# Differential attention: the value split first in each eviction, the weight split ahead of the second exponential, and weight buffers as rings of single pools

## The chip, the core and the metric

The kernel runs on one core of a Trainium2 chip. The metric is device time of one execution in microseconds; the time before is 2284.65 us, the median of 3 runs (2283.86 to 2284.76). PE stands for TensorE, DVE for VectorE, ACT for ScalarE, POOL for GpSimd, SP for the engine that issues most DMAs. Each engine works through its own instructions in the order in which the program has them; an instruction that waits holds up those behind it on its engine.

## The reference

One decoder layer over 1024 positions of width 1024: a normalised input h feeds three branches (mLSTM, differential attention, cross-attention into 256 memory tokens), whose outputs are projected, gated by sigmoids of h, merged, projected again and added to the input; then a squared-ReLU MLP. The change lies mostly in the second branch, and beside it in where the mLSTM branch and the gates keep their weights.

```python
def diff_attention(q, k, v, q_g, k_g, lam, subln_g, lam_init):
    q = rms_norm(q, q_g)
    k = rms_norm(k, k_g)
    ...
        s = jnp.einsum('bhcqd,bhckd->bhcqk', qblk, kt).astype(jnp.float32) * scale
        s = jnp.where(kpos[None, :] <= qpos[:, None], s, -jnp.inf)
        p = jax.nn.softmax(s, axis=-1)
        a = p[:, :, 0] - lam * p[:, :, 1]
        return jnp.einsum('bhqk,bhkv->bhqv', a.astype(vt.dtype), vt)
    ...
    o = rms_norm(o, subln_g) * (1.0 - lam_init)
```

There are 8 heads; each has two query-key pairs (c = 0 and 1) of 64 columns and values of 128 columns, and the two softmaxes are subtracted with the learned weight lam.

## The kernel before

**Precision.** Every matmul operand is split into a high half in fp32r (a cast on ACT) and a low half (source minus high half, a subtraction on DVE); a product takes three matmuls (high-high, high-low, low-high). So each weight tile, each transposed probability tile and each value tile costs one ACT instruction and one DVE instruction, the second behind the first. `split2` emits such a pair.

**Stages.** Normalisation and memory keys, cross-attention, mLSTM (four heads, 25 weight buffers w, 3 load buffers raw), 96 gate steps of their own (14 weight buffers, 2 load buffers), the attention branch, the rest of the gates, then output projections and the MLP.

**The attention branch (`branch_d`).** Its order is written out by hand and kept on PE, DVE and ACT. Three streams are woven together:

- The projection stream (`d_gemm`) is a generator. One token tile (128 rows by 384 columns: q, k and v of a head) takes 8 steps of three matmuls into one of two PSUM banks (mm). With the eighth step comes `evict`: ACT copies q and k out of the bank (draw, 128x512 with each column block doubled), squares them (dscr) and casts v's high half (dv). The remainder waits in the list `after`: DVE subtracts v's low half out of the bank, then sums the squares (drr). After four tiles POOL makes the reciprocal roots, and `turns` gives four pieces of work: PE transposes the rows of q (twice) and k (twice) into the *other* mm bank (pr), ACT and DVE split the result (dq, dk, dkl). Between the second and third, DVE scales k (four multiplies of draw by drr).
- The attention stream runs in slots s = 0 to 68. A slot computes scores of query block s for c = 0 (PE: sc; DVE: mask and maximum in one instruction, then dst; ACT: the exponential dpe), calls `after()`, combines the two exponentials of block s - 1 on DVE (dpe), runs 4 projection steps, the value products of block s - 2 (po), a piece of `turns`, one more projection step, the scores for c = 1, then the transposes of block s - 1 (tp) whose halves daT are split by ACT and DVE, the second exponential, and the last three projection steps. A head is eight slots, since a block attends to one to eight key blocks. The doS tiles hold the outputs, normalised every four blocks.
- The weight stream (`ahead`) loads and splits a weight of the next head, at the end of each slot: one in six of the eight slots, none in the seventh, two in the eighth. In the last head it loads gate weights instead.

The eighth projection step is the last one of a slot, so an eviction always falls at the slot's end, right before `ahead`.

A tile pool with several buffers is one region of memory: when the pools of a stage are closed and the next stage's are opened over them, a new tile waits for what lies beneath it. `Ring` hands out tiles of several pools in strict turn; before, it is used by the last stages only.

Of the kernel before, what the change touches and what calls it, by code (L numbers as in the profile page):

```python
# [17 lines left out]
P = 128  # L18
# [13 lines left out]
def f32(ap):  # L32
    return ap.bitcast(F32)
# [38 lines left out]
class Layer:  # L72
# [9 lines left out]

    pinned = False
    nmm, kmm = 0, 2
# [17 lines left out]
    def split2(self, hi, lo, src):  # L102

        self.A.copy(hi, src)  # L104
        self.V.tensor_sub(lo, src, f32(hi))  # L105

# [10 lines left out]
    def mm3(self, out, l, r, first, last):  # L117

        mm = self.mm
        mm(out, l[0], r[0], start=first, stop=False)  # L120
        mm(out, l[0], r[1], start=False, stop=False)
        mm(out, l[1], r[0], start=False, stop=last)

    def rsqrt_mean(self, r, ss, width, n):
# [756 lines left out]
    def d_gemm(self, pool, kv):  # L881
# [40 lines left out]

        def evict(ps, i, raws, vh, rr):
            rw = pool.tile([P, 4, 2, 64], F32, tag="draw", name=self.name("draw"))
            A.copy(rw, ps[:, 0:256].rearrange("p (a d) -> p a d", a=4).unsqueeze(2).broadcast_to([P, 4, 2, 64]))
            scr = pool.tile([P, 256], F32, tag="dscr", name=self.name("dscr"))
            A.activation(scr, ps[:, 0:256], AF.Square)
            v = pool.tile([P, 2, P], F32R, tag="dv", name=self.name("dv"))
            A.copy(v[:, 0], ps[:, 256:384])
            raws.append(rw)  # L930
            vh.append(v)

            def rest():
                V.tensor_sub(v[:, 1], ps[:, 256:384], f32(v[:, 0]))
                V.tensor_reduce(rr[:, i], scr.rearrange("p (a d) -> p a d", a=4), axis=AX.X, op=ALU.add)
                if i == 3:
                    rl = rr.rearrange("p a b -> p (a b)")
                    self.rsqrt_mean(rl, rl, 64, 16)
                    self.prep = turns(raws, rr, vh)

            self.after.append(rest)
# [16 lines left out]
    def branch_d(self, pool, dw):  # L958
# [19 lines left out]
        def ahead(tile):  # L978
            for _ in range((1, 1, 1, 1, 1, 1, 0, 2)[tile % 8]):
                if next(dw, 0) is not None:  # L980
                    if self.gate_n < 7 * NK:
                        self.gate_load()
                elif len(self.dw.get(7, ())) == NK:
                    self.gate_fetch(6 * NK)

        def scores(s, c):
# [108 lines left out]
        for n in range(8):  # L1095
            fill(1)
            after()
            fill(3)
            p = self.prep.pop(0) if self.prep else None
            if p:  # L1100
                p[0]()
            fill(4)
            if p:
                p[1]()
            ahead(n)
        for s in range(NS + 5):
# [20 lines left out]
            if more:  # L1127
                exp = scores(s, 1)
            if 1 <= s <= NS:
                hi, lo = turn(s - 1, 0)  # L1130
                hi()
                if more:
                    exp()
                fill(1)
                lo()
                if (s - 1) % 8 >= 4:
                    hi, lo = turn(s - 1, 1)
                    hi()
                    lo()
            else:  # L1140
                if more:
                    exp()
                fill(1)
            fill(2)
            if p:
                p[1]()
            ahead(s)
            if 2 <= s < NS + 2 and i == 3:
# [501 lines left out]
    def run(self):  # L1650
        tc, nc = self.tc, self.nc
        with ExitStack() as ctx:
# [22 lines left out]
            with ExitStack() as c1:  # L1675
# [6 lines left out]
                with ExitStack() as c2:  # L1682
# [11 lines left out]
                    with tc.tile_pool(name="pc", bufs=2) as pc, tc.tile_pool(name="pc1", bufs=1) as pc1, tc.tile_pool(name="pc3", bufs=3) as pc3, tc.tile_pool(name="pc4", bufs=6) as pc4, tc.tile_pool(name="wpc", bufs=8) as self.gwp, tc.tile_pool(name="rpc", bufs=2) as self.grp:  # L1694
# [5 lines left out]
                        self.branch_c(T2())  # L1700
                with tc.tile_pool(name="wpm", bufs=25) as self.wp, tc.tile_pool(name="rpm", bufs=3) as self.rp, tc.tile_pool(name="gm", bufs=1) as gm, tc.tile_pool(name="pm1", bufs=1) as pm1, tc.tile_pool(name="pm", bufs=2) as pm, tc.tile_pool(name="pm3", bufs=3) as pm3:
                    class T3:
                        def tile(_, shape, dt, tag, name):
                            p = pm3 if tag == "pre" else pm if tag in ("tho", "cv", "Ch", "C", "hss", "den") else pm1
                            return p.tile(shape, dt, tag=tag, name=name)
                    self.gpool, self.gwp, self.grp = T3(), self.wp, self.rp
                    self.branch_m(T3(), gm, 1)
                with tc.tile_pool(name="wpg", bufs=14) as self.wp, tc.tile_pool(name="rpg", bufs=2) as self.rp:
                    self.gwp, self.grp = self.wp, self.rp
# [6 lines left out]
                    with tc.tile_pool(name="pd", bufs=2) as pd, tc.tile_pool(name="pd3", bufs=3) as pd3, tc.tile_pool(name="pdm", bufs=1) as pdm, tc.tile_pool(name="pd5", bufs=7) as pd5, tc.tile_pool(name="pdv", bufs=5) as pdv, tc.tile_pool(name="pdv2", bufs=17) as pdv2, tc.tile_pool(name="pd4", bufs=4) as pd4:  # L1716
                        self.tmask = pdm.tile([P, D], F32, name="tmask")
                        nc.gpsimd.memset(self.tmask, 0.0)
# [83 lines left out]
```

## Time and profile before

The profiled execution took 2289.52 us, of which the span of its instructions is 2287.7 us; it is 0.2% over the median of the runs. The page's first part gives the busy time of the engines over that span:

| engine | busy us | share | instructions |
|---|---|---|---|
| PE | 2190.8 | 96% | 11222 |
| DVE | 1395.6 | 61% | 2627 |
| ACT | 1010.7 | 44% | 1994 |
| POOL | 553.7 | 24% | 696 |

By stage (start and end in us of the span): mLSTM 180 to 564, gates 564 to about 640, attention branch with its first projections up to about 1197, the remaining gates to about 1220, projections and MLP to the end. In a row of the timeline stand the start, the duration, engine, line, operation, output and inputs with shapes, the number of instructions merged into it, and in brackets how long the engine had been idle before and what released it. A row of waits gives the waiting instruction, the one it waited for, the sum, the number of times and the longest in us.

### The profile page before, as it was taken

What the parts mean: (1) busy time and instruction counts of PE and PEld (TensorE: products, weight loads), DVE (VectorE), ACT (ScalarE), POOL (GpSimd) and SP (SyncE); (2) the same over time, 40 slices, a digit from 0 to 9 for tenths busy, and PEclk for the clock granted to TensorE, in tenths of its full rate; (3) what the DMA queues carried; (4) which work ended last, traced back from release to release, by engine and by line L of the source; (5) the groups of instructions that cost most, each with busy time, mean ns of one, the idle gap of its engine ahead of it and who ended that gap; (6) DMA issues with size and microseconds to landing.
All of it is one profiled execution on the core that took longest, in us unless ns stands there. A gap on an engine that the chain in (4) does not pass through costs nothing.

```text
span 2287.7 us, 30543 instructions
## 1 busy us (share of the span) xinstructions
PE 2190.8 (96%) x11222; PEld 1881.3 (82%) x11222; DVE 1395.6 (61%) x2627; ACT 1010.7 (44%) x1994; POOL 553.7 (24%) x696
## 2 busy tenths in 40 slices
PE   7999999999999999999999999999999999899999
PEld 5788789888898888988887888887787888688777
DVE  6635457553137777777753133453588777766678
ACT  6533445443246666666553111223445444542332
POOL 2100000000011111111100002202566665565553
PEclk9999999999999999999999999999999999899999
DMA  6023212211311111110125344435535444854344
GB/s 242 24 79 97 80 52 79 77 35 48 126 44 33 30 34 38 31 38 23 39 87 190 115 126 137 148 107 178 175 110 194 153 153 151 303 175 151 126 142 166
DMA packets 113780, 247.89 MB, mean 108 GB/s; under 512 B 11065, under 2 KB 19550, under 8 KB 111582
## 3 DMA queue, kind: packets, MB, share of 16 engines
q1 hardware_dynamic: 111326, 233.36, 31.1%
q10 hardware_dynamic: 2304, 12.58, 1.3%
q8 instruction: 88, 1.44, 0.3%
q14 instruction: 62, 0.51, 0.1%
HBM read 178.76 MB, written 67.14 MB: 107 GB/s over the span
## 4 chain that ended last, share of the span: by engine, by line
PE 59%; DVE 18%; DMA 9%; ACT 8%; issue 3%; POOL 2%; SPq 0%; ACTq 0%; DVEq 0%; POOLq 0%
PE mm L91 35%; PE p L91 18%; DVE sc L67 3%; PE sc L91 3%; ACT dpe L67 3%; DVE dst L67 2%; PE tp L94 1%; DMA wraw<-in_wdown 1%; DVE dpe L67 1%; DVE w L67 1%; DVE wo L105 1%; PE po L91 1%; DMA xd<-r_d 1%; DMA kraw<-y 1%; ACT draw L67 1%
## 5 line engine op out<-in xcount | busy, mean ns | idle before, releaser
L91 PE MATMUL mm<-hT,w 128*128 128x512 f32 x1920 | 465.1, 396 | 3.5 <-ACT w L104 2.7
L91 PE MATMUL mm<-w,hT 128*128 128x384 f32 (+3 forms) x2496 | 459.8, 331 | 2.5 <-ACT w L111 2.2
L91 PEld LDWEIGHTS mm<-hT,w 128*128 128x128 f32 x1920 | 354.4, 189 | 79.5 <-ACT w L104 4.3
L91 PEld LDWEIGHTS mm<-w,hT 128*128 128x128 f32 x2496 | 390.6, 189 | 12.1 <-ACT w L111 2.8
L91 PE MATMUL p<-xd,wo 128*128 128x512 f32 x1344 | 314.2, 395 | 16.9 <-DVE acc L1598 9.4
L91 PEld LDWEIGHTS p<-xd,wo 128*128 128x128 f32 x1344 | 254.2, 190 | 76.8 <-DVE acc L1598 12.3
L91 PE MATMUL p<-xo,wo 128*128 128x512 f32 x1344 | 310.0, 392 | 6.0 <-DVE st L1452 4.0
L91 PEld LDWEIGHTS p<-xo,wo 128*128 128x128 f32 x1344 | 253.5, 189 | 61.1 <-ACT pt L1265 4.4
L91 PE MATMUL mm<-kt,w 128*128 128x512 f32 x1152 | 261.6, 389 | 0.5 <-DVE w L112 0.5
L91 PEld LDWEIGHTS mm<-kt,w 128*128 128x128 f32 x1152 | 216.1, 188 | 46.0 <-DVE w L112 1.0
L104 ACT CAST wo<-wraw 128x896 fp32r<-128x896 f32 x122 | 114.9, 942 | 189.7 <-PE p L91 116.8
L105 DVE TENSOR_TENSOR wo<-wraw,wo 128x896 fp32r<-128x896 f32 x122 | 145.9, 1211 | 49.8 <-ACT wo L104 49.7
L67 ACT ACTIVATE dpe<-sc,dst,drr 128x256 f32<-128x256 f32 (+7 forms) x128 | 106.5, 832 | 139.5 <-DVE dst L67 139.3
L1179 POOL TENSOR_TENSOR wraw<-wraw 128x128 f32<-128x128 f32 x128 | 98.1, 766 | 211.4 <-DMA wraw<-in_wdown 132.9
L111 ACT CAST w<-raw 128x256 fp32r<-128x256 f32 (+2 forms) x144 | 86.6, 620 | 132.1 <-PE mm L91 116.3
L112 DVE TENSOR_TENSOR w<-raw,w 128x256 fp32r<-128x256 f32 (+2 forms) x144 | 100.7, 719 | 49.1 <-ACT w L111 48.9
L105 DVE TENSOR_TENSOR xd<-xd 128x1536 fp32r<-128x1536 f32 (+2 forms) x36 | 69.1, 1924 | 72.3 <-ACT xd L104 72.0
L1180 POOL TENSOR_TENSOR wraw<-wraw 128x128 f32<-128x128 f32 x128 | 101.1, 790 | 0.0
L127 POOL TENSOR_SCALAR hss<-hss 128x4 f32<-128x4 f32 x8 | 3.3, 410 | 396.5 <-ACT mscr L755 273.5
L67 DVE CUSTOM_DVE_ANT_0 sc<-sc,tmask 128x256 f32<-128x256 f32 (+7 forms) x128 | 97.0, 758 | 3.0 <-PE sc L91 2.4
L67 DVE TENSOR_TENSOR w<-raw,w 128x384 fp32r<-128x384 f32 (+1 forms) x88 | 44.0, 508 | 85.1 <-ACT w L67 85.0
L1181 POOL TENSOR_TENSOR wraw<-wraw 128x128 f32<-128x128 f32 x128 | 92.8, 725 | 0.0
(324 smaller groups left out, 3187.4 us busy)
## 6 DMA issues: line engine op xcount, KB each, us to landing
wraw<-in_wup SPq DMA_DIRECT2D x64, 256.0 KB, 3.2
r_d<-xts SPq DMA_DIRECT2D x16, 1024.0 KB, 4.3
wraw<-in_wdown SPq DMA_DIRECT2D x64, 256.0 KB, 3.0
xd<-r_d SPq DMA_DIRECT2D x19, 768.0 KB, 7.1
xd<-r_d SPq DMA_DIRECT2D x14, 1024.0 KB, 6.5
raw<-in_wgate SPq DMA_DIRECT2D x48, 256.0 KB, 3.1
gates<-gt SPq DMA_DIRECT2D x48, 256.0 KB, 2.0
raw<-in_wd SPq DMA_DIRECT2D x32, 384.0 KB, 3.1
```

What stands on the lines that cost most here:

```text
L67: return self.tc.keep_in_program_order(f(*a, **k))
L91: self.pin(self.nc.tensor.matmul(out, l, r, start=start, stop=stop))
L94: self.pin(self.nc.tensor.transpose(out, x, self.ident))
L104: self.A.copy(hi, src)
L105: self.V.tensor_sub(lo, src, f32(hi))
L111: nc.scalar.copy(hi, src)
L112: nc.vector.tensor_sub(lo, src, f32(hi))
L127: g.tensor_scalar(r, ss, 1.0 / width, EPS, op0=ALU.mult, op1=ALU.add)
L1179: G.tensor_add(r[:, 4], r[:, 0], r[:, 3])
L1180: G.tensor_sub(r[:, 5], r[:, 4], r[:, 1])
L1181: G.tensor_sub(r[:, 6], r[:, 1], r[:, 0])
```

## The change

In `evict`, the value tile is split first, cast and subtraction together, before q and k are copied and squared; the subtraction is no longer in `after`. In a slot, `ahead` moves from the end to before the second exponential; from there until after the probability tile's low half, the low halves that `split2` would emit are collected (`defer`) and emitted by `lows`. In the eight slots that only project, `ahead` moves two steps forward. The weight and load buffers of mLSTM and of the gates become rings of pools with one buffer each; for the gates they are opened as load buffers, mask, weights, with the weights handed out from the other end, and the mask of the attention branch lies in that group.

```diff
     def split2(self, hi, lo, src):

         self.A.copy(hi, src)
-        self.V.tensor_sub(lo, src, f32(hi))
+        low = lambda: self.V.tensor_sub(lo, src, f32(hi))
+        if self.defer is None:
+            low()
+        else:
+            self.defer.append(low)
...
+    @contextmanager
+    def rings(self, *spec):
+
+        with ExitStack() as c:
+            yield [
+                Ring([c.enter_context(self.tc.tile_pool(name=f"{n}{i}", bufs=1)) for i in range(k)]) for n, k in spec
+            ]
...
         def evict(ps, i, raws, vh, rr):
+            v = pool.tile([P, 2, P], F32R, tag="dv", name=self.name("dv"))
+            self.split2(v[:, 0], v[:, 1], ps[:, 256:384])
             rw = pool.tile([P, 4, 2, 64], F32, tag="draw", name=self.name("draw"))
             A.copy(rw, ps[:, 0:256].rearrange("p (a d) -> p a d", a=4).unsqueeze(2).broadcast_to([P, 4, 2, 64]))
             scr = pool.tile([P, 256], F32, tag="dscr", name=self.name("dscr"))
             A.activation(scr, ps[:, 0:256], AF.Square)
-            v = pool.tile([P, 2, P], F32R, tag="dv", name=self.name("dv"))
-            A.copy(v[:, 0], ps[:, 256:384])
             raws.append(rw)
             vh.append(v)

             def rest():
-                V.tensor_sub(v[:, 1], ps[:, 256:384], f32(v[:, 0]))
                 V.tensor_reduce(rr[:, i], scr.rearrange("p (a d) -> p a d", a=4), axis=AX.X, op=ALU.add)
...
+        def lows():
+            d, self.defer = self.defer, None
+            for f in d:
+                f()
...
-            fill(4)
+            fill(2)
+            ahead(n)
+            fill(2)
             if p:
                 p[1]()
-            ahead(n)
...
+            self.defer = []
             if 1 <= s <= NS:
                 hi, lo = turn(s - 1, 0)
                 hi()
+                ahead(s)
                 if more:
                     exp()
                 fill(1)
                 lo()
+                lows()
                 if (s - 1) % 8 >= 4:
                     hi, lo = turn(s - 1, 1)
                     hi()
                     lo()
             else:
+                ahead(s)
                 if more:
                     exp()
                 fill(1)
+                lows()
             fill(2)
             if p:
                 p[1]()
-            ahead(s)
...
-                with tc.tile_pool(name="wpm", bufs=25) as self.wp, tc.tile_pool(name="rpm", bufs=3) as self.rp, ...
+                with self.rings(("wpm", 25), ("rpm", 3)) as (self.wp, self.rp), ...
...
-                with tc.tile_pool(name="wpg", bufs=14) as self.wp, tc.tile_pool(name="rpg", bufs=2) as self.rp:
+                with self.rings(("rpg", 2), ("ptm", 1), ("wpg", 14)) as (self.rp, ptm, self.wp):
+                    self.wp.pools.reverse()
...
-                        self.tmask = pdm.tile([P, D], F32, name="tmask")
+                        self.tmask = ptm.tile([P, D], F32, name="tmask")
```

On DVE, in the slot of the attention loop that splits a daT tile of 384 columns (ISA is the mask maximum with its read-out; sc the scores, dst the maxima and sums, dpe the exponentials, w a weight, dv the value tile, drr the sums of squares). Before:

```order
L67 TENSOR_TENSOR daT_8905<-tp_8901,daT_8905 128x384
L67 TENSOR_TENSOR w_8924<-raw_8676,w_8924 128x384
L67 ISA sc_8930,dst_8929<-sc_8930,tmask 128x640
L67 ISA dst_8929 128x1
L67 SCALAR_TENSOR_TENSOR dst_8929<-dst_8929,drr_8204 128x1
L67 TENSOR_TENSOR dv_8922<-mm_8865,dv_8922 128x128
L67 TENSOR_REDUCE drr_8590<-dscr_8920 128x4
L67 RECIPROCAL dst_8853<-dst_8853 128x2
```

and now:

```order
L67 TENSOR_TENSOR daT_9054<-tp_9050,daT_9054 128x384
L67 TENSOR_TENSOR w_9056<-raw_8800,w_9056 128x384
L67 TENSOR_TENSOR dv_9070<-mm_9014,dv_9070 128x128
L67 ISA sc_9080,dst_9079<-sc_9080,tmask 128x640
L67 ISA dst_9079 128x1
L67 SCALAR_TENSOR_TENSOR dst_9079<-dst_9079,drr_8353 128x1
L67 TENSOR_REDUCE drr_8739<-dscr_9075 128x4
L67 RECIPROCAL dst_9003<-dst_9003 128x2
```

The value tile's subtraction has moved from behind the mask maximum to ahead of it; the weight's subtraction keeps its place, though its cast on ACT now comes earlier.

On ACT, in the same slot (doS is an output tile, dk a transposed key tile). Before:

```order
L67 CAST daT_8905<-tp_8901 128x384
L67 ACTIVATE dpe_8852,dst_8853<-sc_8896,dst_8853,drr_7846 128x512
L67 COPY draw_8918<-mm_8865 128x512
L67 ACTIVATE dscr_8920<-mm_8865 128x256
L67 CAST dv_8922<-mm_8865 128x128
L67 CAST w_8924<-raw_8676 128x384
L67 ACTIVATE dpe_8927,dst_8929<-sc_8930,dst_8929,drr_8204 128x640
```

and now:

```order
L67 CAST daT_9054<-tp_9050 128x384
L67 CAST w_9056<-raw_8800 128x384
L67 ACTIVATE dpe_9002,dst_9003<-sc_9045,dst_9003,drr_7995 128x512
L67 CAST dv_9070<-mm_9014 128x128
L67 COPY draw_9073<-mm_9014 128x512
L67 ACTIVATE dscr_9075<-mm_9014 128x256
L67 ACTIVATE dpe_9077,dst_9079<-sc_9080,dst_9079,drr_8353 128x640
```

The weight's cast stands ahead of the second exponential, and the value tile is cast before q and k are copied. In the new program the copy draw waits for DVE's subtraction of the value tile.

On ACT, where mLSTM's last head ends and the first gate weights of the next stage are cast (tho is the output gate, Ch the state's high half, gt a gate tile). Before:

```order
L779 ACTIVATE tho_5324<-mm_5299 128x512
L111 CAST Ch_5382<-C_5380 128x258
L750 ACTIVATE den_5385<-sc_5370 128x1
L753 ACTIVATE hS_5368<-sc_5370,den_5385 128x256
L755 ACTIVATE mscr_5390,hss_5369<-hS_5368 128x256
L111 CAST Ch_5416<-C_5414 128x258
```

and now:

```order
L791 ACTIVATE tho_5402<-mm_5377 128x512
L104 CAST w_5744<-raw_5740 128x256
L104 CAST w_5747<-raw_5740 128x256
L104 CAST w_5752<-raw_5742 128x256
L104 CAST w_5755<-raw_5742 128x256
L115 CAST Ch_5460<-C_5458 128x258
L762 ACTIVATE den_5463<-sc_5448 128x1
L765 ACTIVATE hS_5446<-sc_5448,den_5463 128x256
```

The casts of the gate weights, which stood 20 rows later behind the stage's last gate tiles, have moved in between the last output gate and the last chunks' state; on DVE their subtractions stand likewise ahead of the state update C.

More of the change, by code (lines that the diff above doesn't have):

```diff
@@ L1 @@
 import math
-from contextlib import ExitStack
+from contextlib import ExitStack, contextmanager
 import numpy as np
@@ L80, in name @@
         return f"{s}_{self.n}"
-    pinned = False
+    pinned, defer = False, None
     nmm, kmm = 0, 2
@@ L1700, in run @@
                         self.branch_c(T2())
-                with tc.tile_pool(name="wpm", bufs=25) as self.wp, tc.tile_pool(name="rpm", bufs=3) as self.rp, tc.tile_pool(name="gm", bufs=1) as gm, tc.tile_pool(name="pm1", bufs=1) as pm1, tc.tile_pool(name="pm", bufs=2) as pm, tc.tile_pool(name="pm3", bufs=3) as pm3:
+                with self.rings(("wpm", 25), ("rpm", 3)) as (self.wp, self.rp), tc.tile_pool(name="gm", bufs=1) as gm, tc.tile_pool(name="pm1", bufs=1) as pm1, tc.tile_pool(name="pm", bufs=2) as pm, tc.tile_pool(name="pm3", bufs=3) as pm3:
                     class T3:
```

## The prediction

> **What bounds the kernel now.** I read the page's busy shares first, then busy time by stretch, then what TensorE (PE) waited for in the attention stage, then its order of time.
>
> ```profile
> PE 2190.8 (96%) x11222; PEld 1881.3 (82%) x11222; DVE 1395.6 (61%) x2627; ACT 1010.7 (44%) x1994; POOL 553.7 (24%) x696
> ...
> core 0: us, PE busy (x) PEld busy (x) DVE busy (x) ACT busy (x) POOL busy (x), PEclk, DMA share, GB/s
> 250.00:564.00 314.00, 311.53 (x1828) 273.71 (x1829) 172.70 (x431) 147.76 (x409) 12.20 (x16) 0.99 0.19 60
> 564.00:575.00 11.00, 8.20 (x37) 5.49 (x36) 4.33 (x10) 4.98 (x11) 0.47 (x1) 1.00 0.63 187
> 675.00:1135.00 460.00, 429.88 (x2768) 411.86 (x2767) 358.32 (x973) 283.08 (x685) 70.97 (x55) 1.00 0.11 33
> 1480.00:2287.00 807.00, 776.00 (x3367) 633.25 (x3365) 570.20 (x639) 324.59 (x401) 412.92 (x540) 0.98 0.48 163
> ...
> PE pr L94 <- DVE dv L67: 28.6, 39, 1.0
> PE tp L94 <- DVE doS L67: 3.2, 8, 0.5
> PE mm L91 <- ACT w L104: 2.7, 2, 2.4
> ```
>
> PE is busy for 2190.8 of 2287.7 us, so all the idle that any reordering can win back is 96.9 us. The stretches say where it lies: 30.1 us in the differential-attention loop (460.00 - 429.88), 2.8 us where mLSTM hands over to the gates (564 to 575), 2.5 us inside mLSTM, 31 us in the output projections and MLP, which the diff does not touch. In the attention loop PE's clock is 1.00, so it is stalls and not throttling. The three waits name them: 39 times the transposes of q or k (pr) stand until VectorE (DVE) has finished the low half of v, 28.6 us in all; 8 times the transposes of the weights (tp) stand for DVE's doS, 3.2 us; twice the gates' matmuls stand for a weight cast, 2.7 us. One slot in order of time shows why v is late (ACT is ScalarE; the mask maximum is sc<-sc,tmask):
>
> ```profile
> 889.57 0.55 DVE L67 TENSOR_TENSOR daT<-tp,daT 128x384 fp32r<-128x384 f32 x1
> 889.75 0.78 ACT L67 ACTIVATE dpe<-sc,dst,drr 128x512 f32<-128x512 f32 x1 [1.12 <-DVE dst L67]
> 890.42 0.19 ACT L67 ACTIVATION_READ_ACCUMULATOR dpe<-sc,dst,drr 128x1 f32 x1
> 890.51 0.57 ACT L67 COPY draw<-mm 128x512 f32<-128x512 f32 x1
> 890.98 0.39 ACT L67 ACTIVATE dscr<-mm 128x256 f32<-128x256 f32 x1
> 891.25 0.27 ACT L67 CAST dv<-mm 128x128 fp32r<-128x128 f32 x1
> 891.40 0.54 ACT L67 CAST w<-raw 128x384 fp32r<-128x384 f32 x1
> 891.98 0.56 DVE L67 TENSOR_TENSOR w<-raw,w 128x384 fp32r<-128x384 f32 x1 [1.86 <-ACT w L67]
> 892.29 0.80 PE L91 MATMUL po<-dv,daT 128*128 128x256 f32 x6
> 892.45 0.82 DVE L67 CUSTOM_DVE_ANT_0 sc<-sc,tmask 128x640 f32<-128x640 f32 x1
> 893.45 0.28 DVE L67 TENSOR_TENSOR dv<-mm,dv 128x128 fp32r<-128x128 f32 x1
> 893.88 0.63 PE L94 MATMUL pr<-ident,draw 128*128 128x128 f32 x4 [0.78 <-DVE dv L67]
> 894.42 0.75 DVE L67 SCALAR_TENSOR_TENSOR dpe<-dpe,dst,dpe 128x512 f32<-128x512 f32 x1
> 895.93 0.63 PE L94 MATMUL tp<-ident,dpe 128*128 128x128 f32 x4
> ```
>
> ACT drains the finished bank in the order draw, dscr, v, then casts a weight. DVE, in order, idles 1.86 us for that cast, subtracts the weight, does the mask maximum, and only then reads v's low half out of the bank (893.45 to 893.73). PE has ended its value products at 893.09 and needs that same bank for pr: 0.78 us lost.
>
> **Attention loop, part by part.** No instruction is added or removed; their order changes. *Weight split ahead of the second exponential.* ACT sat idle 1.12 us before that exponential (waiting for DVE's dst), the cast takes 0.54 us: it costs nothing on ACT while that gap exceeds 0.54 us, and at most the 0.54 us beyond it. Its subtraction (0.56) follows daT on DVE: 889.57 + 0.55 = 890.12, done by about 890.65, in DVE's former 1.86 us of idle. Its weight load is issued from the same step; SP's order in this loop is unchanged, so no load is passed. *Value first.* v's cast takes draw's place, 890.51 to 890.78; its subtraction follows, about 890.84 to 891.12 (gaps of some 0.06, as between the 891.40 cast's end and 891.98). The mask maximum then starts at about 891.05 instead of 892.45, 1.4 us sooner, and the chain behind it, which also loses v's place in the middle (about 0.2), brings the combination (dpe) from 894.42 to about 892.8. In exchange draw waits for the subtraction, as the new program's waits show: 891.18 instead of 890.51, 0.67 us later; dscr ends near 892.05. The bank is free at 892.05 instead of 893.73, before PE's 893.09. The whole 0.78 us goes here, and the next thing PE needs, tp, would come at 895.93 - 0.78 = 895.15, with its operand ready at 892.8 + 0.75 = 893.6.
>
> The Trainium skill, PSUM — Partial Sum Buffer, section "PSUM bank collisions raise a hardware error", states that ACT and DVE must be kept apart on one bank, two reads included; by that rule the split's round trip through DVE is a price of the change (rival B). Were the two reads allowed together, draw would start at 890.78 here and the sum would stay, since pr is then bound by PE's 893.09; no run here shows such an overlap.
>
> Not each slot has this room. In a slot that also scales k, DVE has four multiplies:
>
> ```profile
> 875.36 1.42 DVE L67 TENSOR_TENSOR draw<-draw,drr 128x256 f32<-128x256 f32 x4
> 877.35 0.56 DVE L67 TENSOR_TENSOR w<-raw,w 128x384 fp32r<-128x384 f32 x1 [0.57 <-ACT w L67]
> 877.82 0.56 DVE L67 CUSTOM_DVE_ANT_0 sc<-sc,tmask 128x384 f32<-128x384 f32 x1
> 878.98 0.63 PE L94 MATMUL pr<-ident,draw 128*128 128x128 f32 x4 [0.76 <-DVE dv L67]
> 879.52 0.48 DVE L67 SCALAR_TENSOR_TENSOR dpe<-dpe,dst,dpe 128x256 f32<-128x256 f32 x1
> 880.32 0.38 PE L94 MATMUL tp<-ident,dpe 128*128 128x128 f32 x2
> ```
>
> Now weight and v come first, then the multiplies (about 876.4 to 877.85), then the maximum at about 877.8, as before. Only v's 0.2 us leaves the chain: the combination ends near 879.8 instead of 880.00. With pr unblocked PE would want tp at 880.32 - 0.76 = 879.56, so some 0.25 us of this wait comes back at tp. Two slots of each eight-slot head are of this kind: 16 x 0.25 = 4.0 us. The doS wait stands in the last slot of a head,
>
> ```profile
> 930.22 0.66 PE L94 MATMUL tp<-ident,dpe 128*128 128x128 f32 x4 [0.38 <-DVE doS L67]
> ```
>
> behind the same late maximum (there DVE subtracts two weights), so it goes too. Sum for the loop: 28.6 + 3.2 - 4.0 = 27.8 us. Bounds: 31.8 (nothing comes back) and about 12 (rival A).
>
> **mLSTM to gates.** Before, the first gate weights could not be loaded until PE was done with the stage; single buffers let them start when the two or three buffers beneath are free, by the program's waits after the last output-gate tile.
>
> ```profile
> 537.99 0.60 ACT L779 ACTIVATE tho<-mm 128x512 f32<-128x512 f32 x1 [4.31 <-PE mm L91]
> 541.09 0.48 DVE L743 SCALAR_TENSOR_TENSOR C<-C,g_dec,sc 128x258 f32<-128x258 f32 x1 [6.68 <-PE sc L91]
> 544.39 0.52 PE L91 MATMUL sc<-Ch,qp 128*128 128x258 f32 x3
> 564.14 0.33 SPq L435 DMA_DIRECT2D raw<-in_wgate  x1
> 567.39 2.12 PE L91 MATMUL mm<-hT,w 128*128 128x512 f32 x8 [2.40 <-ACT w L104]
> 569.77 30.50 PE L91 MATMUL mm<-hT,w 128*128 128x512 f32 x130 [0.26 <-ACT w L104]
> ...
> raw<-in_wgate SPq DMA_DIRECT2D x48, 256.0 KB, 3.1
> ...
> L104 ACT CAST w<-raw 128x256 fp32r<-128x256 f32 x64 | 23.3, 404 | 21.1 <-DMA raw<-in_wgate 18.2 <-PE mm L91 2.9
> ```
>
> The load moves from 564.14 to about 537.8, so PE's 2.40 + 0.26 = 2.7 us go. But the casts and their subtractions now stand ahead of the state update C and its cast Ch: landing 3.1 us after 537.8, four splits of 0.4 us end near 542.7, C slips from 541.09 to 542.7 and Ch's low half is ready near 544.1, against PE's 544.39. The next update, behind four more splits, misses by perhaps 0.3 us. I take 0.7 us given back, net 2.0 (bounds: 2.7 gained, 1.0 lost if landings take 1 us longer twice).
>
> **Inside mLSTM** the buffers now come round in strict turn. The order differs only at the first head switch: eight weight casts move from among the state chunks to behind the tile that last uses the old weights.
>
> ```profile
> 283.14 0.57 ACT L640 COPY pre<-mm 128x512 f32<-128x512 f32 x1
> ...
> 302.13 0.58 ACT L640 COPY pre<-mm 128x512 f32<-128x512 f32 x1
> ```
>
> The first row drains that last tile, the second the first tile of the new weights. At PE's pace of about 0.24 us a matmul (2.12 us for eight overlapping ones, above) its 24 matmuls and the chunks between them begin near 294, so the casts have some 10 us in hand: zero, bounds 0 to 3 us lost. The mask's own pool and one load moved by a place behind the loop touch no wait of PE: zero.
>
> **Sum.** 27.8 + 2.0 = 29.8 us. The profiled execution took 2289.52 us (2287.7 of span and 1.8 around it), 4.9 us over the median of the runs; it should become 2259.7, and the median 2284.65 - 29.8 = **2255 us**.
>
> **Rivals.** *A: the combination takes the wait's place.* If the DVE chain does not move forward, PE stops at tp instead of pr and keeps only the slack that stood before tp: 0.32 us in the k-scaling slot (880.32 against 879.52 + 0.48), 0.76 in the other. At 0.3 us for each of 39 waits that is 12 us, with the 2.0 of the handover 2284.65 - 14 = 2271 us. For it: in the k-scaling slots exactly this holds. Against it: DVE's 1.86 us of idle ahead of the maximum. *B, slower: the round trip of v.* ACT's draw stands for DVE's subtraction, and dscr, the first exponential and pr stand behind draw. The price is the 0.67 us above in each of 64 slots, 43 us, against 31.8 us of waits gone: 2284.65 + 43 - 32 - 2 = 2294 us. It decides only from the point where dscr ends after PE's value products, 1.0 us later than the walk has it (892.05 against 893.09); DVE would have to be that much further behind at each eviction, and the walk finds it free. *C: PE's stalls go, but the handover and the ring cost their bounds* (1.0 and 3 us lost): 2284.65 - 27.8 + 4 = 2261. *D: the order does not do what it says*: excluded for the place of the casts, which the program fixes.
>
> **How the numbers follow.** Forecast (24 to 34 us gained, C included) 0.80; A and halfway to it 0.13; B 0.03; no change for a reason not seen 0.02; more than 34 us, if removing a stall also saves PE's restart, 0.02. The forecast's own range is 2250 to 2261; reaching towards A until no more than 0.2 is left out, and with a little beyond the upper bound of the gain, 2249 to 2268. A measurement of this kernel tells about 0.2% (4.6 us) from no change: faster 0.95, same 0.02, slower 0.03.
>
> **What would show it.** Right: the pr waits for dv near zero, DVE's idle for ACT w in this loop mostly gone, a head taking some 60 us instead of 64, small tp waits for dpe in two slots a head, no 2.4 us wait for a gate weight, PE idle 1 to 5 us in the loop. Wrong: pr waiting for ACT's dscr (B), tp waiting for dpe in most slots (A), waits for Ch or mpT before 564, or ACT's weight casts waiting for their loads, which would hold every exponential behind them.

## The result, and the profile after

The changed kernel takes 2249.8 us (median of 4 runs, 2249.61 to 2250.31), beside 2284.7 us (2283.86 to 2287.53) for the kernel before: 34.9 us less, a ratio of 0.9845 with an interval of 0.9828 to 0.9863. The prediction was 2255 us, with 2249 to 2268 as its range. So the direction and most of the size came as forecast (29.8 of 34.9 us). Two things did not: the gain is 5.1 us larger than the sum, and the experiments put it on another half of the change than the sum's working did.

The busy shares of the page and then the busy time in the attention loop after the change, with the same columns as before (length, PE, PEld, DVE, ACT and POOL busy with their counts, granted clock, DMA share, GB/s):

```profile
PE 2182.6 (97%) x11222; PEld 1877.5 (84%) x11222; DVE 1398.3 (62%) x2627; ACT 1019.8 (45%) x1994; POOL 540.4 (24%) x696
```

```profile
651.71:1107.66 455.95, 453.06 (x2932) 436.22 (x2931) 377.05 (x1017) 304.34 (x719) 66.72 (x60) 1.00 0.12 35
```

This stretch, called the loop below, runs from the first transposition of q or k (pr) to the last. The same stretch of the kernel before:

```profile
653.31:1144.18 490.87, 458.95 (x2931) 438.45 (x2932) 374.00 (x1017) 296.27 (x719) 75.69 (x60) 1.00 0.12 33
```

The loop is 34.92 us shorter. 29.03 us of this is PE's idle time (31.92 before, 2.89 after: length less busy time). The other 5.89 us is PE's *busy* time, 458.95 against 453.06, for the same matmuls at the same clock. What PE still waits for in this loop:

```profile
PE tp L94 <- DVE dpe L67: 1.6, 7, 0.2
PE tp L94 <- DVE doS L67: 1.3, 6, 0.3
```

No pr wait is left, and no wait of the gates' matmuls for a weight cast (before 28.6 and 2.7 us). A head now takes 59.5 us in place of 64.3 (from the value products of one slot to those of the same slot of the next head). One slot in order of time, the one that the prediction walked through; its value products (po) start at 871.95 here and at 892.29 before:

```profile
868.17 0.52 ACT L67 CAST w<-raw 128x384 fp32r<-128x384 f32 x1
869.23 0.78 ACT L67 ACTIVATE dpe<-sc,dst,drr 128x512 f32<-128x512 f32 x1 [0.54 <-DVE dst L67]
869.52 0.55 DVE L67 TENSOR_TENSOR w<-raw,w 128x384 fp32r<-128x384 f32 x1
870.00 0.25 ACT L67 CAST dv<-mm 128x128 fp32r<-128x128 f32 x1
870.29 0.29 DVE L67 TENSOR_TENSOR dv<-mm,dv 128x128 fp32r<-128x128 f32 x1 [0.22 <-ACT dv L67]
870.49 0.82 DVE L67 CUSTOM_DVE_ANT_0 sc<-sc,tmask 128x640 f32<-128x640 f32 x1
870.61 0.59 ACT L67 COPY draw<-mm 128x512 f32<-128x512 f32 x1 [0.36 <-DVE dv L67]
871.95 0.80 PE L91 MATMUL po<-dv,daT 128*128 128x256 f32 x6
872.30 0.78 DVE L67 SCALAR_TENSOR_TENSOR dpe<-dpe,dst,dpe 128x512 f32<-128x512 f32 x1
872.59 0.62 PE L94 MATMUL pr<-ident,draw 128*128 128x128 f32 x4
874.65 0.62 PE L94 MATMUL tp<-ident,dpe 128*128 128x128 f32 x4
```

Counted from po's start, the mask maximum comes at -1.46 us (before +0.16), the combination of the exponentials at +0.35 (before +2.13), pr at +0.64 (before +1.59). The weight's cast fits into ACT's gap ahead of the second exponential: the gap is 0.54 us where it was 1.12. The order of events is the predicted one. But pr came 0.95 us sooner, and the wait shown for it before was only 0.78. The rest is overlap: po ends at 871.95 + 0.80 = 872.75 by its row, and pr starts 0.16 us ahead of that end, where before it started 0.78 us behind it.

### The profile page after: what moved, and what is told of

Same layout as the page of the kernel before. It is cut to its first block, busy times and chain, and to the rows that moved or that the text cites. A ratio compares the mean times of both kernels' runs of the same rounds, so it can differ in the third digit from the quotient of the medians.

```text
span 2247.8 us, 30530 instructions
## 1 busy us (share of the span) xinstructions
PE 2182.6 (97%) x11222; PEld 1877.5 (84%) x11222; DVE 1398.3 (62%) x2627; ACT 1019.8 (45%) x1994; POOL 540.4 (24%) x696
## 4 chain that ended last, share of the span: by engine, by line
PE 68%; DVE 14%; DMA 8%; ACT 5%; issue 2%; POOL 2%; SPq 0%; DVEq 0%; ACTq 0%; POOLq 0%
PE mm L91 40%; PE p L91 18%; PE sc L91 4%; PE tp L94 2%; PE po L91 2%; DVE sc L67 1%; DMA wraw<-in_wdown 1%; ACT dpe L67 1%; DVE wo L105 1%; DVE dpe L67 1%; PE pr L94 1%; DVE draw L67 1%; DVE dst L67 1%; DMA xr<-h_d 1%; DVE w L116 1%
## 5 line engine op out<-in xcount | busy, mean ns | idle before, releaser
L104 ACT CAST xd<-xd 128x1536 fp32r<-128x1536 f32 (+2 forms) x36 | 54.9, 1528 | 73.0 <-DMA xd<-r_d 73.0
```

## The experiments

Times of one kernel spread over 2.6 to 14 us from run to run in these comparisons, so kernels that differ by less than some 4 us are not told apart by their times. The length of the loop in the trace, from the first pr to the last, repeats much better: 490.87, 491.51 and 490.89 us in three kernels with the loop of before, and 455.95, 456.01, 455.69 and 455.67 us in four with the changed loop. It is the main reading in what follows (the times come from several comparisons, each with its own runs of the kernel before; the ratios in the text are taken within one):

| kernel | loop us | PE idle in it | PE busy in it | waits of pr and tp listed in it | time us |
|---|---|---|---|---|---|
| before | 490.87 | 31.92 | 458.95 | pr 39, tp 7 | 2284.7 |
| value split first alone | 511.37 | 45.43 | 465.94 | pr 1, tp 43 | 2301.8 |
| value cast first alone | 490.89 | 31.94 | 458.95 | pr 39, tp 7 | 2284.6 |
| weight split early alone | 452.27 | 0.61 | 451.66 | none | 2246.0 |
| the change | 455.95 | 2.89 | 453.06 | tp 13 | 2249.8 |
| the change, value's subtraction late | 452.50 | 0.75 | 451.75 | none | 2245.1 |
| the change, value last | 474.43 | 14.73 | 459.70 | tp 20 | 2260.5 |
| the change, k scaled one slot sooner | 450.84 | 0.41 | 450.43 | tp 1 | 2240.2 |

The list of waits holds those of 0.15 us and more. The eighth doS wait of the kernel before (0.32 us at 1210.82) lies behind the loop.

### Each half of the attention change alone

The kernel before, with only the value split moved:

```diff
         def evict(ps, i, raws, vh, rr):
+            v = pool.tile([P, 2, P], F32R, tag="dv", name=self.name("dv"))
+            self.split2(v[:, 0], v[:, 1], ps[:, 256:384])
             rw = pool.tile(...)
...
             def rest():
-                V.tensor_sub(v[:, 1], ps[:, 256:384], f32(v[:, 0]))
```

> The kernel before with the value split first alone: cast and subtraction at once, before q and k are copied; the weight split stays at the slot's end. Theory (the late weight split holds the mask maximum, the early value only frees the bank): pr no longer waits for dv, but the combination is no earlier than before (0.2 us sooner without the value in its chain, some 0.3 later since the weight cast now follows the round trip), so PE stops at tp and keeps only the slack of 0.3 us in most of 39 slots: about 2273 us (2268 to 2277), with some 20 us of tp waits. Rival (the bank alone held PE): 2252 us and hardly a tp wait.

Measured: 2301.82 us (2300.47 to 2303.28), ratio 1.0079 (1.0061 to 1.0098): slower than the kernel before of the same comparison (2283.11), by 18.7 us. The expectation of 2273 fell, and its rival of 2252 with it. Its waits of PE in the attention loop:

```profile
PE tp L94 <- DVE dpe L67: 26.3, 30, 1.2
PE tp L94 <- DVE doS L67: 18.7, 13, 2.1
```

The pr waits are gone and 45.0 us of tp waits stand in their place. The same slot in this kernel, one head sooner:

```profile
827.95 0.29 DVE L67 TENSOR_TENSOR dv<-mm,dv 128x128 fp32r<-128x128 f32 x1 [0.69 <-ACT dv L67]
828.27 0.59 ACT L67 COPY draw<-mm 128x512 f32<-128x512 f32 x1 [0.36 <-DVE dv L67]
829.03 0.52 ACT L67 CAST w<-raw 128x384 fp32r<-128x384 f32 x1
829.22 0.80 PE L91 MATMUL po<-dv,daT 128*128 128x256 f32 x6
829.58 0.56 DVE L67 TENSOR_TENSOR w<-raw,w 128x384 fp32r<-128x384 f32 x1 [1.34 <-ACT w L67]
829.86 0.62 PE L94 MATMUL pr<-ident,draw 128*128 128x128 f32 x4
830.05 0.82 DVE L67 CUSTOM_DVE_ANT_0 sc<-sc,tmask 128x640 f32<-128x640 f32 x1
832.93 0.66 PE L94 MATMUL tp<-ident,dpe 128*128 128x128 f32 x4 [0.86 <-DVE doS L67]
```

pr follows po by 0.64 us, unhindered. But the mask maximum comes at +0.83 us after po's start, 0.67 later than before (+0.16). DVE still waits 1.34 us for the weight's cast, which ACT now makes behind the eviction *and* behind the round trip of v, and the mask maximum stands behind the weight's subtraction. tp comes at +3.71, where it came at +3.64 before and at +2.70 in the changed kernel. This is rival A, the combination taking the wait's place, with rival B's round trip on top, paid not at pr but at tp.

This slot is hardly longer for it: from po to the next po it takes 8.54 us, beside 8.47 before. The loss lies in others. The slot behind it, which had no wait before, goes from 7.83 to 8.56 us; the last slot of a head, where two weights are split, goes from 9.53 to 10.2 us, with a tp wait of 2.1. In four of these seven last slots it is 11.8 us instead, at a granted clock of 0.86 (1066.06 to 1077.84), beside 10.2 us at 1.00 (863.56 to 873.75): 4 x 1.6 = 6.4 of the 20.5 us that the loop is longer are clock. Each of these dips follows a tp wait of 2.1 us, but two such waits (734.44 and 868.93) are followed by none, so what brings them is not shown.

The other half, everything of the change in the slot loop (`ahead` moved, `defer`, `lows`) with `evict` and the pools as they were:

> The kernel before with the weight split ahead of the second exponential alone: value last in the eviction, its subtraction behind the mask maximum as before. Theory: the maximum starts some 1.8 us sooner, so the subtraction behind it also ends before PE's value products in most slots; only the two k-scaling slots of a head keep about 0.3 us: 2254 to 2258 us, pr waits of about 5 us. Rival (the value's place decides): the pr waits stay near 28 us and the time near 2284 us.

Measured: 2246.02 us (2240.06 to 2249.75), ratio 0.9833 (0.9808 to 0.9858). It carries the whole gain of the loop. The expectation, 2254 to 2258 us with 5 us of pr waits, was too slow: the k-scaling slots keep no wait either. The loop, in which the trace lists no wait:

```profile
649.22:1101.49 452.27, 451.66 (x2932) 437.00 (x2931) 374.45 (x1016) 300.17 (x719) 75.63 (x60) 1.00 0.12 35
```

In its walked slot:

```profile
864.71 0.55 DVE L67 TENSOR_TENSOR w<-raw,w 128x384 fp32r<-128x384 f32 x1
...
865.50 0.83 DVE L67 CUSTOM_DVE_ANT_0 sc<-sc,tmask 128x640 f32<-128x640 f32 x1 [0.24 <-PE sc L91]
...
866.50 0.28 DVE L67 TENSOR_TENSOR dv<-mm,dv 128x128 fp32r<-128x128 f32 x1
...
867.43 0.80 PE L91 MATMUL po<-dv,daT 128*128 128x256 f32 x6
```

With the weight's subtraction out of the way, the mask maximum starts 1.93 us ahead of po and now waits for PE's scores. v's subtraction, still behind it, is done at 866.78, ahead of po's start and 1.29 us ahead of pr (868.07). The value never had to go first: it was late only because the mask maximum ahead of it was late, and that because of the weight. That the change is slower than this half alone rests on the loops (455.95 against 452.27; 455.69 in the change with the old pools, below); the times do not tell them apart.

### The value's place, with the weight early

Three kernels vary the place of the value. In the first, ACT casts v first as in the change, and DVE subtracts in `after` again:

```diff
-            self.split2(v[:, 0], v[:, 1], ps[:, 256:384])
+            A.copy(v[:, 0], ps[:, 256:384])
...
             def rest():
+                V.tensor_sub(v[:, 1], ps[:, 256:384], f32(v[:, 0]))
```

> The changed kernel with the value's cast first but its subtraction back behind the mask maximum, so draw waits for no other engine. Theory (what counts is that DVE no longer waits for a weight cast): the subtraction still ends ahead of pr except in the k-scaling slots, 2252 to 2256 us, pr waits 2 to 6 us. Rival (the subtraction must stand ahead of the maximum): 2265 us or more.

2245.06 us (2242.21 to 2249.13), ratio 0.9832 (0.9816 to 0.9849); loop 452.50 us, no wait listed. The 2252 to 2256 us with 2 to 6 us of pr waits that were expected did not come, nor did the rival's 2265. The same as the weight alone: the 3.5 us between this and the change's 455.95 are what the immediate subtraction costs.

In the second, v is split last in the eviction, with its subtraction at once:

```diff
         def evict(ps, i, raws, vh, rr):
-            v = pool.tile([P, 2, P], F32R, tag="dv", name=self.name("dv"))
-            self.split2(v[:, 0], v[:, 1], ps[:, 256:384])
...
             A.activation(scr, ps[:, 0:256], AF.Square)
+            v = pool.tile([P, 2, P], F32R, tag="dv", name=self.name("dv"))
+            self.split2(v[:, 0], v[:, 1], ps[:, 256:384])
```

> The changed kernel with the eviction in the order draw, dscr, value: cast and subtraction together but last, so no copy waits for DVE, and the maximum waits for the value's cast. Theory: the maximum starts some 0.7 us later than in the changed kernel; slots with slack hide it, the k-scaling slots and a few others lose 0.5 to 0.9 us at tp: 2258 to 2265 us with 8 to 14 us of tp waits. Rival (the round trip of draw through DVE is what costs): faster than 2249.8 us.

2260.46 us (2256.86 to 2262.07), ratio 0.9892 (0.9877 to 0.9907), as expected; loop 474.43 us. Two rows of a slot, and then its waits of PE in this loop:

```profile
888.03 0.29 DVE L67 TENSOR_TENSOR dv<-mm,dv 128x128 fp32r<-128x128 f32 x1 [0.95 <-ACT dv L67]
888.24 0.96 DVE L67 CUSTOM_DVE_ANT_0 sc<-sc,tmask 128x768 f32<-128x768 f32 x1
```

```profile
PE tp L94 <- DVE dpe L67: 11.0, 14, 1.0
PE tp L94 <- DVE doS L67: 3.2, 6, 0.5
```

A DVE instruction that stands ahead of the mask maximum and waits for ACT delays tp here, v's subtraction as well as the weight's. If the subtraction is to be immediate, v has to be first; if it is late, v may stand first or last.

The last of this kind settles whether ACT's order or DVE's made "value first alone" slow: the kernel before, with ACT's cast of v ahead of draw and nothing else moved.

> Kernel before, with only the cast of v's high half moved ahead of draw on ScalarE; the subtraction of its low half stays behind the mask maximum on VectorE, and the weight split stays behind the evictions. Theory: the place of a VectorE instruction in its order decides, because it stands ahead of the mask maximum; ScalarE's order of the same three drains does not. Without the subtraction between them the three drains and the weight cast end where they did (no 0.67 us round trip), so the mask maximum starts where it did and v's low half is read where it was: first to last q or k transposition 490 to 492 us as in the kernel before (490.87, and 491.51 with the rings), some 39 waits of pr for v's low half, 28 to 29 us in all, time within 5 us of the kernel before. Rival: that splitting the value first alone came out slower lies in ScalarE's order (draw and its square later for every consumer); then this kernel shows the tp waits of that one (some 45 us) and a loop near 511 us.

2284.62 us (2281.74 to 2293.31), ratio 0.9997 (0.9985 to 1.0009); loop 490.89 us, with these waits (of the whole execution, so that the doS wait behind the loop is among them):

```profile
PE pr L94 <- DVE dv L67: 28.6, 39, 1.0
PE tp L94 <- DVE doS L67: 3.0, 8, 0.5
```

The loop is as long as before to 0.02 us, as expected. ACT's order alone changes nothing; the 20.5 us by which the loop of "value first alone" is longer come with DVE's subtraction in the middle of the eviction.

### The k scaling

The change's remaining waits begin in the slot that scales k, where four multiplies stand ahead of the mask maximum:

```profile
857.63 1.42 DVE L67 TENSOR_TENSOR draw<-draw,drr 128x256 f32<-128x256 f32 x4
858.97 0.56 DVE L67 CUSTOM_DVE_ANT_0 sc<-sc,tmask 128x384 f32<-128x384 f32 x1
859.12 0.34 PE L91 MATMUL po<-dv,daT 128*128 128x256 f32 x2
860.48 0.48 DVE L67 SCALAR_TENSOR_TENSOR dpe<-dpe,dst,dpe 128x256 f32<-128x256 f32 x1
861.02 0.44 PE L94 MATMUL tp<-ident,dpe 128*128 128x128 f32 x2 [0.22 <-DVE dpe L67]
```

First edit: the multiplies ahead of the slot's last two projection steps in the program.

```diff
-            fill(2)
             if p:
                 p[1]()
+            fill(2)
```

> The changed kernel with the four k multiplies issued ahead of the last projection steps, so that on DVE they stand ahead of the value's subtraction in two slots of eight; draw then waits some 1.4 us longer. This moves the eviction past the point at which the round trip (rival B) decides. Theory: in the shorter of the two slots dscr ends some 0.7 us after PE's value products, pr waits for ACT; 16 slots lose 0.2 to 0.8 us: 2253 to 2258 us, pr waits of 4 to 7 us. Rival (the round trip is always hidden): 2249 to 2251 us.

2246.4 us (2244.16 to 2250.88), ratio 0.9835 (0.982 to 0.985); loop 455.24 us, 0.7 less than the change: nothing that the time can show. The expected 2253 to 2258 us did not come. The multiplies are as many and still stand ahead of the mask maximum; only v's subtraction changed sides with them. The theory holds in kind, not in size: the 7 tp waits for dpe are gone, and in their place stand 6 waits of pr for ACT's dscr, 1.1 us in all instead of the 4 to 7 expected. So the round trip (rival B) does reach pr once v's subtraction stands 1.4 us later, and costs little there.

Second edit: the multiplies a whole slot sooner, behind the first q piece rather than the second, where sixteen value products give DVE room.

```diff
-            return [(lambda: q_(0), none), (lambda: q_(1), scale), ...
+            return [(lambda: q_(0), scale), (lambda: q_(1), none), ...
```

> The changed kernel with the four k multiplies one slot earlier (with the first q piece instead of the second), into slots whose combination has over 1 us of slack before tp. Theory (a stall costs its shown idle plus about 0.13 us of matmul tail that no longer overlaps): the 7 waits of 0.22 us for dpe go, 7 x 0.35 = 2.5 us: 2247.4 us, provided POOL's roots are done in time. Rival (a stall costs its idle alone): 2248.2 us. Other rival (the multiplies only move the wait): 2249.8 us with 0.2 us waits in other slots.

2240.17 us (2239.2 to 2247.04), ratio 0.9824 (0.9797 to 0.9852). The expected time was 2247.4. The changed kernel again, in the same comparison:

> The changed kernel once more, on the chip of the next two: 2249.8 us (2249 to 2251).

2248.24 us (2247.19 to 2249.78), ratio 0.9853 (0.9822 to 0.9883). The loop of the edit:

```profile
648.02:1098.86 450.84, 450.43 (x2932) 436.30 (x2931) 377.97 (x1017) 304.68 (x719) 66.71 (x60) 1.00 0.12 35
```

5.17 us shorter than the repetition's 456.01, about twice the 2.5 us expected, with one wait of 0.4 us left. The mask maximum of that slot now starts 1.50 us ahead of po, where it started 0.15 ahead. The doS waits of the head's last slot went as well; that they were lag carried over from the k-scaling slot fits this, but was not tested apart. It has the lowest median and the shortest loop here. The intervals of the two ratios overlap, so the gain over the change rests on the loop.

Third, the normalisation of the outputs moved ahead of the value products as well (the call of `norm` in the slot loop):

> The same, and the transposes of the normalised outputs moved ahead of the value products, so that the probability tile no longer takes over the bank of the value products: the 6 waits of 0.21 us for doS go too, 6 x 0.34 = 2.0 us more: 2245.4 us. Rival (idle alone): 2246.9 us.

2240.85 us (2238.34 to 2246.72), ratio 0.9822 (0.9794 to 0.9851); loop 452.39 us, 1.6 more than without this edit, with a new wait of 1.0 us in the last head (a projection matmul for dkl); a doS wait of 0.7 us stands behind the loop. The 2 us more that were expected did not come.

### The rings

The kernel before with the rings alone; the change with the old pools; the change with mLSTM's old pools and only the gates' rings:

```diff
-                with tc.tile_pool(name="wpm", bufs=25) as self.wp, tc.tile_pool(name="rpm", bufs=3) as self.rp, ...
+                with self.rings(("wpm", 25), ("rpm", 3)) as (self.wp, self.rp), ...
```

> The kernel before with the rings alone. Theory: the handover's 2.7 us of waits go, about 1 us comes back as waits for Ch and mpT in mLSTM: 2283 us (2282 to 2284.5), loop waits of 28.6 and 3.2 us unchanged. Rival (the rings carry the gain beyond the loop's shown waits): 2279 us or less.

> The changed kernel with the buffers of mLSTM and gates as the pools of before. Theory: the loop gains all but the handover, 2251.4 us (2250.5 to 2252.5), the 2.4 us wait for the first gate weight is back. Rival (the rings also help or harm elsewhere): more than 2 us away from that.

> The changed kernel with mLSTM's buffers as pools of before and only the gates' buffers as single pools. Theory (both sides of the handover must be single buffers, since a pool is released whole): the wait of PE for the first gate weight is back at about 2.4 us, 2251.4 us. Rival (single gate buffers suffice): no such wait, 2249.8 us or a little less since mLSTM keeps its old order.

Rings alone: 2283.49 us (2275.95 to 2287.1), ratio 0.9995 (0.9982 to 1.0009), no difference that the times show. The change without rings: 2247.88 us (2245.97 to 2255.51), 0.985 (0.9827 to 0.9872). With the gates' rings only: 2249.84 us (2245.58 to 2258.19), 0.9852 (0.9829 to 0.9876). None of the three differs by its time from the kernel that it is derived from, so the traces decide. (The change without rings is also below its expected 2250.5 to 2252.5, but its two waits for the first gate weights are back, 2.6 and 0.5 us, as expected.) First the handover, in the kernel before and then in the changed one (transposition of mLSTM's last outputs, then the gates' matmuls):

```profile
563.95 1.03 PE L94 MATMUL tp<-ident,hS 128*128 128x128 f32 x8
```

```profile
539.31 9.47 SPq L447 DMA_DIRECT2D raw<-in_wgate  x6
...
544.91 0.43 DVE L116 TENSOR_TENSOR Ch<-C,Ch 128x258 fp32r<-128x258 f32 x1 [0.47 <-ACT Ch L115]
547.20 0.52 PE L91 MATMUL sc<-Ch,qp 128*128 128x258 f32 x3
566.76 1.03 PE L94 MATMUL tp<-ident,hS 128*128 128x128 f32 x8
567.55 12.77 PE L91 MATMUL mm<-hT,w 128*128 128x512 f32 x55
```

The load starts at 539.31 instead of 564.14, and the gates' matmuls follow the transposition by 0.79 us instead of 3.44 (567.39 less 563.95). The state is not disturbed: Ch's low half is done at 545.34, PE wants it at 547.20. With the gates' rings alone this does not happen; the load starts at 559.58 (timeline), in a kernel that is 4.6 us ahead of the kernel before at mLSTM's last use of Ch, and PE waits as before (waits):

```profile
559.58 0.33 SPq L447 DMA_DIRECT2D raw<-in_wgate  x1
```

```profile
PE mm L91 <- ACT w L104: 2.4, 1, 2.4
```

The tiles *beneath* must be free one by one; that the tiles on top are single is not enough. Whether mLSTM's rings alone would do was not tested. From mLSTM's last use of Ch to the first pr, five kernels without mLSTM's rings take 100.8 to 101.3 us (a sixth, value cast first, 103.2) and eight with them 96.8 to 97.3: 4.2 us less.

But mLSTM itself gets longer. From its first use of Ch to its last, here in the kernel before and then with the rings alone (first and last start in us):

```profile
L91 PE MATMUL sc<-Ch,qp x84: 276/282/388, 257.9 to 552.0; 128*128 128x258 f32 x84
```

```profile
L91 PE MATMUL sc<-Ch,qp x84: 276/283/387, 256.0 to 553.3; 128*128 128x258 f32 x84
```

294.1 us become 297.3; over these fourteen, 293.8 to 294.1 without and 296.1 to 297.6 with the rings. The place is the first head switch. In the changed kernel:

```profile
306.75 0.51 PE L91 MATMUL sc<-Ch,qp 128*128 128x258 f32 x2 [0.59 <-DVE Ch L116]
...
311.37 0.51 PE L91 MATMUL sc<-Ch,qp 128*128 128x258 f32 x2 [0.38 <-DVE Ch L116]
```

This is where the eight weight casts were moved to. All eight kernels with mLSTM's rings have two to four waits of PE for mpT or Ch here, 43 to 54 us behind the first use of Ch, 0.9 to 2.4 us in all (in the changed kernel 1.2); the six without have none. Both stretches together, from the first Ch to the first pr, take 395.0 us in the mean of those five (395.4 with the sixth) and 394.0 in that of the eight: the rings gain about 1.0 us.

## Why the prediction was right, and where not

**What bounds the kernel** held: PE's stalls in the attention loop, for v's low half, behind a mask maximum that waits for a weight. PE's idle time there went from 31.92 to 2.89 us, where the sum had 31.8 going to 4.0. The gain of 34.9 us lies just above the band of 24 to 34 us to which the forecast gave 0.80, and inside the wider range. DVE's idle time ahead of the weights' subtractions in this loop fell from 63.1 to 2.3 us.

**The size of the loop term was too small**, because a stall was priced at the idle time shown for it. The forecast took 27.8 us and the idle time fell by 29.0, but the loop shrank by 34.9. The missing 5.9 us is PE's busy time. The starts and ends of the single matmuls in the trace show where it comes from. An unhindered matmul starts 0.16 us ahead of the end shown for the one before it; a stalled one starts behind that end, so this overlap is lost on top of the idle time. The first transposition after a stall is longer too: 0.33 us instead of 0.27 at tp, 0.30 instead of 0.29 at pr. A stall therefore costs about 0.18 us at pr and 0.22 at tp beyond its idle time. The loop before has 46 listed stalls and five too short to be listed, that after the change 13 and one: the count gives 6.2 us, and 5.9 were measured. (The ends of matmuls in a profile are modelled, so the division of a stall into idle and busy time is the profile's own; the length of the loop is not.) This had been given 0.02 as "if removing a stall also saves PE's restart"; it decided most of the difference.

**What is given back** was 2.9 us of idle against 4.0 forecast, in other places than said. The size of a tp wait in a k-scaling slot was right (0.23 against 0.25), but only one of the two such slots in a head keeps it, 7 waits instead of 16; the other has ten value products to cover it, not two. The doS wait, which was to go, stayed in 6 of its 7 places in the loop, with 1.3 us in place of 2.9.

**The two edits of the loop were told as two causes, and they are not.** The walk's order of events is right for both together. But it credited the mask maximum's 1.4 us to "value first", and it is the weight's early split that gives them: alone it makes the loop 38.6 us shorter (490.87 to 452.27), while value first alone makes it 20.5 us longer. In the changed kernel the immediate subtraction costs some 3.5 us (455.95 against 452.50). The round trip was sized well: from the start of v's cast to that of draw it is 0.61 us, both in the changed kernel and with value first alone, where the walk had 0.67. What was wrong is that its cost was looked for at pr only (rival B's condition, dscr later than PE's value products). Without the early weight it falls on the next weight cast, the mask maximum and tp, which the slack of 1.0 us ahead of pr says nothing of. The Trainium skill, PSUM — Partial Sum Buffer, section "PSUM bank collisions raise a hardware error", keeps ACT and DVE apart on one bank, two reads included. The trace agrees, in that draw starts at 870.61, 0.03 us after the subtraction's end (870.29 + 0.29), as the program has it wait, and no run here shows the two at once.

**The handover** gained 4.2 us, not 2.7 (2.65 of them at the first gates' matmul), and the 0.7 us feared there for the state update did not come: Ch was ready 1.9 us ahead of PE. **Inside mLSTM** the zero was wrong. The moved casts had been held against the new weights' matmuls, for which they had 10 us in hand; they were not held against the state chunks whose Ch and mpT now stand behind them on ACT and DVE. That costs 2.0 to 3.5 us, within and just over the bound of 3 that rival C also had. Net 1.0 us where 2.0 were forecast.

**The sum** then reads 34.9 for the loop and 1.0 for the rings, 35.9 against 34.9 between the medians; the rest is within their spread. That the total came within 5.1 us is in part luck: the loop was 7.1 us too small and the rings 1.0 us too large. Rivals A and B, which the changed kernel does not show, appeared together when half of the change was left out; D is excluded by the place of the casts in the trace.

**The same count elsewhere.** "Value last" has 8.0 us more busy time than the weight alone (459.70 less 451.66) at 20 listed waits, which looks like 0.4 us each. It is not: another 14 tp groups and ten pr transpositions start late by too little to be listed, and lose the overlap as well. With them the count gives 8.0. "Value first alone" has 14.3 us more: 43 tp stalls make some 9.5, the four clock dips 6.4, and 1.6 go off for 14 short delays of pr in the kernel with the weight alone.

**What stays open**: what brings the clock dips of "value first alone"; whether the doS waits of a head's last slot are lag carried over from the k scaling; and where the rest of the handover's 4.2 us lies.

## What to carry to other kernels

When a consumer waits for an engine that works in order, look at what stands ahead of the late instruction and at what that waits for, and move the instruction that waits for another engine, not the one that is late. Trace an added round trip between two engines to every consumer behind it, not only to the one that the change is meant for. An edit of two halves should be walked once with each half alone: here one half has all the gain of the loop, and the other lengthens it, by 3.7 us with the first half in place and by 20.5 without.

## What the runs showed of the hardware that was not expected

A PE stall costs more than the idle time that the trace shows before the waiting matmul: 0.16 us of overlap with the matmul before it, and up to 0.06 us for a longer first matmul. It is seen as a longer busy time for the same matmuls at a clock of 1.00 (458.95 us with 46 listed stalls, 451.66 with none listed). Delays under 0.15 us are not listed and cost it too. In a loop like this one, with dozens of stalls, the sum of shown waits is a lower bound of what their removal brings.
